# Weighing the values of four query tiles together instead of two, with narrowing matmuls

## Chip, cores and metric

The kernel runs on one core of a Trainium2 chip. The metric is the device time of one execution in microseconds (us), the median of several runs. Engines are named as in the profile: PE (TensorE, matmuls), PEld (its weight loads), DVE (VectorE), ACT (ScalarE), POOL (GpSimd) and SP (SyncE, which issues most DMA transfers).

## What is computed

One layer of a decoder trunk over 1024 tokens of width 1024: a combined input projection, differential attention with 8 heads, a convolution branch, a gated merge and a feed-forward part. The change lies in the attention, whose core is this:

```python
def block(i):                       # 128 queries
    bias = transpose(bias_tab[t5_bucket(rel)], (2, 0, 1))
    causal = rel >= 0
    def probs(qb, kf):
        s = einsum('bhqd,bhkd->bhqk', qb, kf) * scale + bias
        s = where(causal, s, -inf)
        return softmax(s, axis=-1)
    p = probs(qb1, k1f) - lam * probs(qb2, k2f)
    return einsum('bhqk,bhkd->bhqd', p, vf)
...
a = rms_norm(a, subln_w) * (1.0 - lam_init)
y_a = a.reshape(B, S, ATTN_WIDTH) @ w_proj_attn
```

Query tile i (128 queries) sees the key tiles 0 to i only; what lies behind them is masked.

## The kernel before

**Precision.** A product of two fp32 numbers is made in three matmuls: each operand is split into a rounded part ("hi", fp32r) and the rest ("lo"), and `mm3` (lines 168 to 170) adds hi x hi, hi x lo and lo x hi in PSUM. `split_hi` is a copy on ACT (line 120), `split_lo` a subtraction on DVE (line 125).

**The attention stage.** A step is one head h and one query tile i. The 64 steps run head by head, in each of the first seven heads over the tiles 4, 5, 6, 7, 0, 1, 2, 3, and in the last over 6, 7, 4, 5, 2, 3, 0, 1 (`ORDER`). A step n does this:

- `scores` (lines 1289 to 1306): scores of the tile against its keys, bias, exponentials, and the difference of the two softmaxes in the tile E.
- `turn` of the step before: PE transposes E in blocks of 128 x 128 (tile pT), ACT and DVE split the result into ph and pl. ph and pl have one buffer each. A pair of query tiles (b = i // 2) shares them; the block of the pair's last key tile that is masked for the first query tile is set to zero by POOL.
- `weigh`, after the second tile of a pair: V (stationary, 128 x 128, tiles vh and vl) times ph and pl (moving, 256 queries), over 2b + 2 key tiles, into PSUM (pW), and a copy to SBUF by ACT (tile ar).
- `back`, two steps later: PE transposes ar back to queries in rows (pB), and ACT scales it and sums its squares. With the pair that is last in a head, `subln` and, one step on, `subln_T` follow; the result goes to DRAM through the tile "at" (two buffers).
- between them, `more` and `group` issue pieces of the large projections (tile pg; names whi, wlo, hT_hi, hT_lo), which keep PE busy while DVE and ACT work; `turn_qk` turns Q and K of later heads (pQ), whose halves are moved between partitions by DMAs on SP (qs, ks, klo); and one or more convolution taps run on DVE (line 594).

**What sets the order.** The functions are recorded in this order; a scheduler then lists the instructions of each engine, following what depends on what and the explicit `tc.issue_after`. Each engine issues in its listed order. PSUM tiles of the kinds pT, pW, pB, pS and pQ take turns in two pools, `pm` (two buffers) and `pm2` (one buffer).

Of the kernel before, what the change touches and what calls it, by code (L numbers as in the profile page):

```python
# [10 lines left out]
F32 = mybir.dt.float32  # L11
# [5 lines left out]
P = 128  # L17
S = 1024
D = 1024
H = 8  # L20
# [37 lines left out]
def kernel(  # L58
# [28 lines left out]
    dve, act, pool, pe = nc.vector, nc.scalar, nc.gpsimd, nc.tensor  # L87
# [24 lines left out]
    def nm(s):  # L112
        uid[0] += 1
        return f"{s}_{uid[0]}"

    def f32(ap):
        return ap.bitcast(F32)

    def split_hi(dst, src):
        act.copy(dst, src)  # L120
# [3 lines left out]
    def split_lo(dst, src, hi):  # L124
        last_lo[0] = dve.tensor_tensor(dst, src, f32(hi), op=ALU.subtract).ins  # L125
# [9 lines left out]
    def after(ins):  # L135

        return nullcontext() if ins is None else tc.issue_after(ins)

    def last_of(engine):
        for ins in reversed(nc.cur_bb.bb.instructions):  # L140
            if ins.engine == engine:
                return ins
# [19 lines left out]
    def pm(z="pm"):  # L162
        npm[0] += 1
        p_, tag = pms[npm[0] % len(pms)]
        return p_.tile([P, 512], F32, tag=tag, name=nm(z))

    def mm3(o, lh, ll, rh, rl, start, stop):
        pe.matmul(o, lh, rh, start=start, stop=False)  # L168
        pe.matmul(o, lh, rl, start=False, stop=False)  # L169
        last_mm[0] = pe.matmul(o, ll, rh, start=False, stop=stop).ins  # L170
# [47 lines left out]
    at = [0]  # L218
# [556 lines left out]
    def bias_skew(h):  # L775
        pool.dma_start(t_d[h][:], b_d[h : h + 1, :].to_broadcast([P, TL]))
# [89 lines left out]
    def load_bias(h):  # L866
        tb = apl[0].tile([P, S], F32, tag="tb", name=f"tb{h}", bufs=1)
        skew = t_d[h][:].rearrange("p l -> (p l)")[P - 1 : P - 1 + P * (TL - 1)]
        nc.sync.dma_start(tb[:], skew.rearrange("(p l) -> p l", l=TL - 1)[:, :S])
        TB[h] = tb  # L870
# [361 lines left out]
    n = 0  # L1232
# [21 lines left out]
    aps = apl[0]  # L1254
# [4 lines left out]
    V, AN, SSA, PT, ES, RL = {}, {}, {}, {}, {}, {}  # L1259

    def load_v(h):
        vh = aps.tile([P, NT, VD], F32R, tag="vh", name=f"vh{h}", bufs=1)
        vl = aps.tile([P, NT, VD], F32R, tag="vl", name=f"vl{h}", bufs=1)
        for dst, src in ((vh, v_hi[h // 2]), (vl, v_lo[h // 2])):
            nc.sync.dma_start(
                f32(dst[:]),
                src[:, (h % 2) * VD : (h % 2 + 1) * VD].rearrange("(k p) d -> p k d", p=P),
            )
        V[h] = vh, vl
# [39 lines left out]

    ORDER = [(4, 5, 6, 7, 0, 1, 2, 3)] * (H - 1) + [(6, 7, 4, 5, 2, 3, 0, 1)]  # L1310

    def turn(h, i):

        b = i // 2
        if (h, b) not in PT:
            ph = aps.tile([P, NT, 256], F32R, tag="ph", name=nm("ph"), bufs=1)
            pl = aps.tile([P, NT, 256], F32R, tag="pl", name=nm("pl"), bufs=1)
            pool.memset(f32(ph[:, 2 * b + 1, 0:P]), 0.0)
            pool.memset(f32(pl[:, 2 * b + 1, 0:P]), 0.0)
            PT[h, b] = ph, pl  # L1320
        ph, pl = PT[h, b]
        e = ES.pop((h, i))
        qs = slice((i % 2) * P, (i % 2 + 1) * P)
        for k0 in range(0, i + 1, 4):
            n = min(4, i + 1 - k0)
            pt = pm("pT")
            for k in range(n):
                pe.transpose(pt[:, k * P : (k + 1) * P], e[:, (k0 + k) * P : (k0 + k + 1) * P], ident[:])  # L1328
            src = pt[:, : n * P].rearrange("p (k q) -> p k q", q=P)
            split_hi(ph[:, k0 : k0 + n, qs], src)  # L1330
            split_lo(pl[:, k0 : k0 + n, qs], src, ph[:, k0 : k0 + n, qs])

    def weigh(h, b):

        ph, pl = PT.pop((h, b))
        vh, vl = V[h]
        o = pm("pW")
        nkt = 2 * b + 2
        for k in range(nkt):
            mm3(o[:, :256], vh[:, k, :], vl[:, k, :], ph[:, k, :], pl[:, k, :], k == 0, k == nkt - 1)  # L1340
        ar = aps.tile([P, 256], F32, tag="ar", name=nm("ar"), bufs=1)
        act.copy(ar[:], o[:, :256])
        return ar

    def back(h, b, ar):
        pt = pm("pB")
        for e in range(2):
            pe.transpose(pt[:, e * P : (e + 1) * P], ar[:, e * P : (e + 1) * P], ident[:])
        if h not in AN:
            AN[h] = aps.tile([P, NT, VD], F32, tag="an", name=f"an{h}", bufs=1)  # L1350
            SSA[h] = sm.tile([P, NT], F32, tag="ssa", name=nm("ssa"))
        jk = sm.tile([P, VD], F32, tag="jk", name=nm("jk"), bufs=1)
        for e in range(2):
            i = 2 * b + e
            src, r = pt[:, e * P : (e + 1) * P], RL[h][:, i, 0:1]
            act.activation(AN[h][:, i, :], src, AF.Identity, scale=r)
            act.activation(jk[:], src, AF.Square, scale=r, accum_out=SSA[h][:, i : i + 1])

    def subln(h):
        an = AN[h]  # L1360
        r = rstd_of(SSA[h][:], NT, 1.0 / VD, fast=True)
        dve.tensor_tensor(an[:], an[:], r.unsqueeze(2).to_broadcast([P, NT, VD]), op=ALU.mult)

    def subln_T(h):
        an = AN[h]
        for sb in range(2):
            pt = pm("pS")
            for i in range(4):
                pe.transpose(pt[:, i * P : (i + 1) * P], an[:, 4 * sb + i, :], ident[:])
            if h == H - 1:  # L1370

                hi, lo = [a_[-1][:, sb * 512 : (sb + 1) * 512] for a_ in (aT_hi, aT_lo)]
                act.activation(hi, pt[:], AF.Identity, scale=pcol("subln"))
                dve.scalar_tensor_tensor(lo, pt[:], pcol("subln"), f32(hi), op0=ALU.mult, op1=ALU.subtract)
                continue
            at = aps.tile([P, 512], F32, tag="at", name=nm("at"), bufs=2)
            act.activation(at[:], pt[:], AF.Identity, scale=pcol("subln"))
            nc.sync.dma_start(a_d[h][:, sb * 512 : (sb + 1) * 512], at[:])
# [9 lines left out]
    scm, weighs, backs, sublns = [], [], [], []  # L1388
# [3 lines left out]
    def more(k):  # L1392

        with after(scm[-4] if len(scm) >= 4 else None):
            for _ in range(k):
                next(fill, None)
        last_fill[0] = last_mm[0]
# [8 lines left out]
    def ready(queue, n):  # L1406
        now = [e for e in queue if e[0] <= n]
        queue[:] = [e for e in queue if e[0] > n]
        return [e[1] for e in now]

    def slot(n, nq):

        with after(last_fill[0]):
            for h, b, ar in ready(backs, n):
                back(h, b, ar)
                if b == ORDER[h][-1] // 2:
                    subln(h)
                    sublns.append((n + 1, h))
            for _ in range(min(nq, 2)):
                if late[0][0] <= n:  # L1420
                    late.pop(0)[1]()
            for h in ready(sublns, n):
                subln_T(h)
            for h, b in ready(weighs, n):
                backs.append((n + 2, (h, b, weigh(h, b))))
                if b == ORDER[h][-1] // 2 and h + 1 < H:
                    load_v(h + 1)

    def groups(n):

        return 0 if plan[n // NT] == 6 and n % NT in (4, 6) or n == len(steps) - 1 else 1
# [14 lines left out]
    for n, (h, i) in enumerate(steps):  # L1446
        if n % NT == 0 and h:
            load_bias(h)
        if n % NT == 2 and h + 2 < H:
            with after(last_of(mybir.EngineType.Pool)):  # L1450
                bias_skew(h + 2)
        p = groups(n)
        nq = len(late)
        scores(h, i)
        scm.append(last_mm[0])
        more((p + 1) // 2)
        if n:
            hp, ip = steps[n - 1]
            turn(hp, ip)
            if ip % 2:  # L1460
                weighs.append((n, (hp, ip // 2)))
        more(p // 2)
        slot(n, nq)
        due += share * slack[n]
        with after(last_of(mybir.EngineType.DVE)):
            bg.step(int(due + 1e-6))
        due -= int(due + 1e-6)
    n = len(steps)
# [63 lines left out]
    for h in (5, 6):  # L1532
        for sb in range(2):
            cs = slice(sb * 512, (sb + 1) * 512)
            at = bp.tile([P, 512], F32, tag="ya", name=f"at{h}_{sb}", bufs=4)[:]
# [145 lines left out]
    for cl in ((0, 1, 2), (3, 4), (5, 6), (7,)):  # L1681
        pair = [(c, ws.next()) for c in cl]
        for sb in range(2):
            cs = slice(sb * 512, (sb + 1) * 512)
            for c, w in pair:
# [3 lines left out]
                o = gemm_T(w, cT_hi, cT_lo, sb)  # L1689
# [63 lines left out]
    for z, tag in enumerate(("xhi", "xlo")):  # L1753
        t_ = f32(big.tile([P, NKT, S], F32R, tag=tag, name=f"room{z}")[:])
# [37 lines left out]
    o = {}  # L1792
    for z, (z_, b_, s_, (l, c), full) in enumerate(WSEVEN):
# [21 lines left out]
        for j in range(4):  # L1815
# [24 lines left out]
            for i in range(4):  # L1840
                t_ = slice(i * P, (i + 1) * P)
# [17 lines left out]
        for i in range(4):  # L1859
            t_ = 4 * l + i  # L1860
            h = xa[t_][:, TOK[c]]
# [273 lines left out]
```

## Time and profile before

| | us |
|---|---|
| median of 3 runs | 1727.08 |
| lowest and highest run | 1726.94 and 1728.37 |
| span of the profiled execution, first to last instruction | 1725.7 |
| attention stage, about 306 to 822 in the span | 516 |
| PE busy over the span | 1714.6 |
| DVE busy over the span | 1275.4 |
| ACT busy over the span | 862.5 |

The profiled execution has no time of its own beside its span. A row of the groups reads: line, engine, operation, output <- inputs by tile name, shape, count, then total busy us, mean ns of one, and idle time before it with what ended it. A row of the timeline reads: start in us, duration in us, engine, line, operation, names, shape. PE's durations overlap, so that the distance between starts tells what a matmul costs in a stream.

### The profile page before, as it was taken

How to read it: one execution, taken by the hardware profiler on the slowest of the kernel's cores; microseconds unless marked ns; L12 is line 12 of the kernel's file. 1: busy time of each engine (PE TensorE's matmuls, PEld its weight loads, DVE VectorE, ACT ScalarE, POOL GpSimd, SP SyncE). 2: the span in 40 equal slices, each digit the busy share in tenths (PEclk: the TensorE clock that was granted, in tenths of full speed). 3: DMA queues.
4: the chain of work that ended last, by engine and by line, in shares of the span. 5: the costliest groups of instructions: out<-in, count | busy, mean ns of one | idle time of the engine just before them, and what ended most of it. 6: DMA issues, size and time to landing. Idle time of an engine off the chain costs nothing.

```text
span 1725.7 us, 25863 instructions
## 1 busy us (share of the span) xinstructions
PE 1714.6 (99%) x9243; PEld 1477.9 (86%) x9243; DVE 1275.4 (74%) x2128; ACT 862.5 (50%) x1958; POOL 219.1 (13%) x207
## 2 busy tenths in 40 slices
PE   9999999999999999999999999999999999999999
PEld 7997889998998998988788888888888888888887
DVE  7675889898988888878687769966676666575544
ACT  5333335767777776756556325633333333333332
POOL 3997851000000000000000000000000000000000
PEclk9999999999999999999999999999999999999999
DMA  6344445336345344343973683245455445598663
GB/s 208 116 126 132 131 151 154 104 109 171 104 127 147 115 125 138 101 136 130 333 238 118 200 296 119 74 135 164 147 170 170 154 141 164 175 355 285 217 215 130
DMA packets 261604, 281.64 MB, mean 163 GB/s; under 512 B 16546, under 2 KB 181986, under 8 KB 261475
## 3 DMA queue, kind: packets, MB, share of 16 engines
q1 hardware_dynamic: 254160, 267.71, 48.3%
q0 software_dynamic: 5680, 9.39, 2.6%
q10 hardware_dynamic: 1634, 2.89, 0.5%
q8 instruction: 73, 1.20, 0.3%
q14 instruction: 57, 0.46, 0.1%
HBM read 181.84 MB, written 85.50 MB: 155 GB/s over the span
## 4 chain that ended last, share of the span: by engine, by line
PE 92%; DMA 3%; DVE 2%; ACT 1%; issue 1%; POOL 0%; SPq 0%; DVEq 0%; POOLq 0%; ACTq 0%
PE acc L980 29%; PE acc L488 12%; PE pg L168 12%; PE pg L169 12%; PE pg L170 12%; PE wo L1850 3%; PE sc L1290 2%; PE sc L1289 2%; PE pT L1328 2%; PE pg L1106 1%; DVE acc L594 1%; PE pW L168 1%; PE pW L169 1%; PE pW L170 1%; PE pQ L815 1%
## 5 line engine op out<-in xcount | busy, mean ns | idle before, releaser
L594 DVE SCALAR_TENSOR_TENSOR acc<-u,cw,acc 128x1023 f32<-128x1023 f32 (+14 forms) x240 | 303.4, 1264 | 23.2 <-ACT acc L588 20.7
L170 PE MATMUL pg<-whi,hT_lo 128*128 128x256 f32 x704 | 200.2, 285 | 0.0
L168 PE MATMUL pg<-whi,hT_hi 128*128 128x256 f32 x704 | 199.7, 285 | 0.4 <-DVE v L125 0.4
L169 PE MATMUL pg<-wlo,hT_hi 128*128 128x256 f32 x704 | 199.5, 284 | 0.0
L125 DVE TENSOR_TENSOR wlo<-draw,whi 128x1024 fp32r<-128x1024 f32 x75 | 91.7, 1223 | 83.4 <-ACT whi L120 78.9
L120 ACT CAST whi<-draw 128x1024 fp32r<-128x1024 f32 x75 | 79.1, 1055 | 129.5 <-PE acc L488 114.3
L169 PEld LDWEIGHTS pg<-wlo,hT_hi 128*128 128x128 f32 x704 | 134.4, 191 | 1.8
L170 PEld LDWEIGHTS pg<-whi,hT_lo 128*128 128x128 f32 x704 | 134.3, 191 | 1.8
L168 PEld LDWEIGHTS pg<-whi,hT_hi 128*128 128x128 f32 x704 | 134.0, 191 | 2.1 <-DVE v L125 0.6
L120 ACT CAST whi<-wraw 128x1024 fp32r<-128x1024 f32 x90 | 94.7, 1052 | 70.6 <-PE pg L169 32.6
L488 PE MATMUL acc<-wlo,whi 128*128 128x512 f32 x308 | 119.8, 389 | 0.0
L488 PE MATMUL acc<-whi,wlo 128*128 128x512 f32 x308 | 119.8, 389 | 0.0
L1296 ACT ACTIVATE E<-E,mn 128x640 f32<-128x640 f32 (+7 forms) x128 | 99.8, 781 | 30.8 <-DVE mn L1291 29.2
L168 PE MATMUL pg<-hT_hi,whi 128*128 128x512 f32 x288 | 114.4, 397 | 0.1
L169 PE MATMUL pg<-hT_lo,whi 128*128 128x512 f32 x288 | 113.7, 395 | 0.0
L170 PE MATMUL pg<-hT_hi,wlo 128*128 128x512 f32 x288 | 113.7, 395 | 0.0
L120 ACT CAST whi<-s 128x1024 fp32r<-128x1024 f32 x54 | 56.9, 1053 | 104.9 <-PE acc L980 101.8
L125 DVE TENSOR_TENSOR wlo<-wraw,whi 128x1024 fp32r<-128x1024 f32 x75 | 93.3, 1246 | 12.6 <-ACT whi L120 12.3
L1291 DVE CUSTOM_DVE_ANT_0 E<-sc,tb 128x512 f32<-128x512 f32 (+3 forms) x128 | 74.2, 585 | 33.2 <-PE pT L1328 16.1
L980 PE MATMUL acc<-h_hi,whi 128*128 128x512 f32 x240 | 93.4, 389 | 0.0
L980 PE MATMUL acc<-h_lo,whi 128*128 128x512 f32 x240 | 93.4, 389 | 0.0
L980 PE MATMUL acc<-h_hi,wlo 128*128 128x512 f32 x240 | 90.1, 389 | 0.0
(370 smaller groups left out, 4589.7 us busy)
## 6 DMA issues: line engine op xcount, KB each, us to landing
wraw<-in_w_gate_up_dram SPq DMA_DIRECT2D x44, 512.0 KB, 4.7
wraw<-in_w_in_dram SPq DMA_DIRECT2D x38, 512.0 KB, 4.0
qs<-qs SPq DMA_DIRECT2D x96, 128.0 KB, 2.3
wd<-in_w_down_dram SPq DMA_DIRECT2D x44, 256.0 KB, 3.1
tdT<-wd SPq DMA_DIRECT2D x88, 128.0 KB, 4.8
draw<-sdS SPq DMA_DIRECT2D x44, 256.0 KB, 3.7
draw<-tdT SPq DMA_DIRECT2D x44, 256.0 KB, 3.7
wraw<-in_w_in_dram SPq DMA_DIRECT2D x32, 256.0 KB, 3.3
```

The costliest lines, as they stand in the source:

```text
L120: act.copy(dst, src)
L125: last_lo[0] = dve.tensor_tensor(dst, src, f32(hi), op=ALU.subtract).ins
L168: pe.matmul(o, lh, rh, start=start, stop=False)
L169: pe.matmul(o, lh, rl, start=False, stop=False)
L170: last_mm[0] = pe.matmul(o, ll, rh, start=False, stop=stop).ins
L488: m = pe.matmul(o[s_][i][:], l_[:, ts], r_[:, 512:], start=start and j + y_ == 0, stop=j == n - 1 and y_ == 2, skip_group_check=not start,)
L594: dve.scalar_tensor_tensor(a_, us[c][:, : S - n], cw[:, c, t : t + 1], a_, op0=ALU.mult, op1=ALU.add)
L980: last_mm[0] = pe.matmul(o[:], a_[x_][:, k, :], b_[y_][:, k, :], start=start and k + x_ + y_ == 0, stop=k == 3 and x_ == 1, skip_group_che ...
L1289: pe.matmul(o[:, :w], qh[:, qs], k, start=True, stop=False)
L1291: dve.tensor_tensor_reduce(e[:, ks], o[:, :w], tb[:, S - nk + c0 : S - nk + c0 + w], 1.0, mn[:, j : j + 1] if c0 else 3.0e38, ALU.add, ALU ...
L1296: act.activation(e[:, :nk], e[:, :nk], AF.Exp, bias=mn[:, j : j + 1], scale=-1.0, accum_out=l[:, j : j + 1])
L1850: last_mm[0] = pe.matmul(o[s_][i][:], A[u_], B[v_], start=start and j + y_ == 0, stop=j == 3 and y_ == 2, skip_group_check=not start,).ins
```

## The change

For the first seven heads the query tiles 0 to 3 share one ph and one pl, read as 4 key tiles x 512 queries. They are weighed once, after tile 3. Key tile k is seen only by the queries from tile k on, so its matmuls run over 512, 384, 256 and 128 columns and no zeros are needed. The way back is made in two halves, tiles 0 and 1 one step later, 2 and 3 two steps later. The copy of pW goes to a buffer of the tile "at". Tiles 4 to 7, and the last head, stay as they were.

```diff
+    def four(h, i):
+        return i < 4 and h < H - 1
+
     def turn(h, i):
 
-        b = i // 2
+        b = 0 if four(h, i) else i // 2
         if (h, b) not in PT:
             ph = aps.tile([P, NT, 256], F32R, tag="ph", name=nm("ph"), bufs=1)
             pl = aps.tile([P, NT, 256], F32R, tag="pl", name=nm("pl"), bufs=1)
-            pool.memset(f32(ph[:, 2 * b + 1, 0:P]), 0.0)
-            pool.memset(f32(pl[:, 2 * b + 1, 0:P]), 0.0)
+            if four(h, i):
+                ph, pl = [t_[:].rearrange("p k q -> p (k q)").rearrange("p (k q) -> p k q", q=512) for t_ in (ph, pl)]
+            else:
+                pool.memset(f32(ph[:, 2 * b + 1, 0:P]), 0.0)
+                pool.memset(f32(pl[:, 2 * b + 1, 0:P]), 0.0)
             PT[h, b] = ph, pl
         ph, pl = PT[h, b]
         e = ES.pop((h, i))
-        qs = slice((i % 2) * P, (i % 2 + 1) * P)
+        q0 = i if four(h, i) else i % 2
+        qs = slice(q0 * P, (q0 + 1) * P)
...
     def weigh(h, b):
 
-        ph, pl = PT.pop((h, b))
         vh, vl = V[h]
         o = pm("pW")
+        if four(h, 2 * b):
+            ph, pl = PT.pop((h, 0))
+            for k in range(4):
+                qs = slice(k * P, 512)
+                mm3(o[:, qs], vh[:, k, :], vl[:, k, :], ph[:, k, qs], pl[:, k, qs], k == 0, k == 3)
+            ar = aps.tile([P, 512], F32, tag="at", name=nm("ar"), bufs=2)
+            act.copy(ar[:], o[:])
+            return ar
+        ph, pl = PT.pop((h, b))
...
             for h, b in ready(weighs, n):
-                backs.append((n + 2, (h, b, weigh(h, b))))
+                ar = weigh(h, b)
+                if four(h, 2 * b):
+                    backs.append((n + 1, (h, 0, ar[:, 0:256])))
+                    backs.append((n + 2, (h, 1, ar[:, 256:512])))
+                else:
+                    backs.append((n + 2, (h, b, ar)))
...
-            if ip % 2:
+            if ip == 3 or ip % 2 and not four(hp, ip):
                 weighs.append((n, (hp, ip // 2)))
```

What this makes of the order, at two places of the first head. PE before, where the tiles 0 and 1 are weighed (pW_3885), among the scores (sc) of tile 3:

```order
L1289 MATMUL sc_3959<-ks_1_0_3725,qs_1_1_3708 128x512
L168 MATMUL pW_3885<-ph_3808,vh_3156 128x256
L1290 MATMUL sc_3959<-ks_1_0_3725,qs_1_1_3711 128x512
L1289 MATMUL sc_3963<-ks_1_1_3479,qs_1_1_3708 128x128
L1290 MATMUL sc_3963<-ks_1_1_3479,qs_1_1_3711 128x128
L1289 MATMUL sc_3969<-ks_1_0_3726,qs_1_1_3709 128x512
L169 MATMUL pW_3885<-pl_3809,vh_3156 128x256
L170 MATMUL pW_3885<-ph_3808,vl_3157 128x256
L168 MATMUL pW_3885<-ph_3808,vh_3156 128x256
L169 MATMUL pW_3885<-pl_3809,vh_3156 128x256
L170 MATMUL pW_3885<-ph_3808,vl_3157 128x256
L1328 MATMUL pT_3945<-ident,E_3821 128x128 x3
```

PE in the change, where the four tiles are weighed (pW_4065); its first matmul, over ph and 512 columns, stands 18 rows ahead of these:

```order
L169 MATMUL pW_4065<-pl_3809,vh_3156 128x512
L170 MATMUL pW_4065<-ph_3808,vl_3157 128x512
L168 MATMUL pW_4065<-ph_3808,vh_3156 128x384
L169 MATMUL pW_4065<-pl_3809,vh_3156 128x384
L170 MATMUL pW_4065<-ph_3808,vl_3157 128x384
L168 MATMUL pW_4065<-ph_3808,vh_3156 128x256
L169 MATMUL pW_4065<-pl_3809,vh_3156 128x256
L170 MATMUL pW_4065<-ph_3808,vl_3157 128x256
L168 MATMUL pW_4065<-ph_3808,vh_3156 128x128
L169 MATMUL pW_4065<-pl_3809,vh_3156 128x128
L170 MATMUL pW_4065<-ph_3808,vl_3157 128x128
L1289 MATMUL sc_4098<-ks_1_0_3726,qs_1_1_3709 128x512
```

Six matmuls of 256 columns went from the first place, and at the second, where 12 of 256 columns stood before, 12 of four widths stand now. Between the first matmul and these, 17 of a projection (pg) are listed. In all, PE has 42 matmuls fewer: 126 of 256 columns are replaced by 21 each of 512, 384, 256 and 128.

ACT before, from the copy of tiles 0 and 1 (ar_3892) over their way back (pB_4063) to the copy of tiles 2 and 3 (ar_4101):

```order
L1342 COPY ar_3892<-pW_3885 128x256
L120 CAST ph_3941<-pT_3945 128x3x128
L797 COPY qkraw_3995<-pg_4134 128x512
L1296 ACTIVATE E_3958,l_3957<-E_3958,mn_3956 128x640
L120 CAST ph_3941<-pT_4056 128x4x128
L1356 ACTIVATE an_3696<-pB_4063,rl_0_3182 128x128
L1357 ACTIVATE jk_4066,ssa_3697<-pB_4063,rl_0_3182 128x128
```

ACT in the change, from the joint copy to the first half of the way back (pB_4196):

```order
L1350 COPY ar_4078<-pW_4065 128x512
L1296 ACTIVATE E_4087,l_4086<-E_4087,mn_4085 128x768
L120 CAST whi_3976<-wraw_3974 128x1024
L1296 ACTIVATE E_4097,l_4086<-E_4097,mn_4085 128x768
L120 CAST ph_4181<-pT_4185 128x4x128
L120 CAST ph_4181<-pT_4192 128x128
L1371 ACTIVATE an_3696<-pB_4196,rl_0_3182 128x128
L1372 ACTIVATE jk_4199,ssa_3697<-pB_4196,rl_0_3182 128x128
```

One copy of 512 columns stands for two of 256, and the way back of tiles 0 and 1 comes behind the turn of the next head's first tile (pT_4185) instead of behind that of tile 3.

## The prediction

> **What bounds the kernel now.** I read the page first, then the waits of TensorE (PE), then the stage in which the change lies.
>
> ```profile
> span 1725.7 us, 25863 instructions
> PE 1714.6 (99%) x9243; PEld 1477.9 (86%) x9243; DVE 1275.4 (74%) x2128; ACT 862.5 (50%) x1958; POOL 219.1 (13%) x207
> PE   9999999999999999999999999999999999999999
> PEclk9999999999999999999999999999999999999999
> PE 92%; DMA 3%; DVE 2%; ACT 1%; issue 1%; POOL 0%; SPq 0%; DVEq 0%; POOLq 0%; ACTq 0%
> ```
>
> PE is busy in every slice at full clock, and 92% of the chain that ended last is PE. A matmul's busy time includes a modelled end that overlaps the next matmul, so "99%" alone doesn't prove it; the list of what PE waited for does:
>
> ```profile
> PE pm L208 <- DVE busy L195: 1.5, 1, 1.5
> PE sc L1289 <- DMA ks<-klo: 1.1, 1, 1.1
> PE sc L1290 <- DMA qs<-qs: 0.8, 1, 0.8
> PE px L724 <- DVE xt L714: 0.6, 1, 0.6
> ```
>
> The columns are the total wait in us, how often, and the longest. These are the largest; everything else is 0.5 us or less. Only two of them, together 1.9 us, lie in the attention stage:
>
> ```profile
> core 0: us, PE busy (x) PEld busy (x) DVE busy (x) ACT busy (x) POOL busy (x), PEclk, DMA share, GB/s
> 306.00:822.00 516.00, 513.49 (x3417) 468.86 (x3417) 441.57 (x977) 365.38 (x1202) 19.49 (x73) 1.00 0.44 126
> ```
>
> In these 516 us VectorE (DVE) works 441.6 and ScalarE (ACT) 365.4, so both have slack, and PE has next to none. So the time follows the PE work that is issued, counted from one matmul's start to the next one's start, plus any new wait.
>
> **The change, part by part.** First the weighing. Before, each head weighs tiles 0 and 1 with 2 key tiles x 3 = 6 matmuls of 256 columns, and tiles 2 and 3 with 4 x 3 = 12. What one costs:
>
> ```profile
> L168 PE MATMUL pW<-ph,vh 128*128 128x256 f32 x160 | 45.7, 286 | 0.1
> 340.70 0.28 PE L168 MATMUL pW<-ph,vh 128*128 128x256 f32 x1
> 340.82 0.28 PE L169 MATMUL pW<-pl,vh 128*128 128x256 f32 x1
> ...
> 342.74 0.28 PE L170 MATMUL pW<-ph,vl 128*128 128x256 f32 x1
> 342.86 0.60 PE L1328 MATMUL pT<-ident,E 128*128 128x128 f32 x4
> ```
>
> The mean of 286 ns is the time until a result is out, not the price. The 18 matmuls of one weighing start between 340.70 and 342.86: 2.16 us / 18 = 0.120 us each. Removed per head: 18 x 0.120 = **2.16 us**.
>
> The new form has three matmuls each of 512, 384, 256 and 128 columns. pW has none of the other widths, but other matmuls of the same type do:
>
> ```profile
> 929.88 0.39 PE L168 MATMUL pg<-cT_hi,whi 128*128 128x512 f32 x1
> ...
> 932.82 0.39 PE L169 MATMUL pg<-cT_lo,whi 128*128 128x512 f32 x1
> 319.79 0.34 PE L1289 MATMUL sc<-ks,qs 128*128 128x384 f32 x1
> 319.97 0.34 PE L1290 MATMUL sc<-ks,qs 128*128 128x384 f32 x1
> 320.14 0.28 PE L168 MATMUL pg<-whi,hT_hi 128*128 128x256 f32 x1
> 340.02 0.22 PE L1289 MATMUL sc<-ks,qs 128*128 128x128 f32 x1
> 340.08 0.28 PE L1290 MATMUL sc<-ks,qs 128*128 128x128 f32 x1
> 340.19 0.45 PE L168 MATMUL pg<-hT_hi,whi 128*128 128x512 f32 x1
> 340.47 0.39 PE L169 MATMUL pg<-hT_lo,whi 128*128 128x512 f32 x1
> ```
>
> 512 columns: the two rows are the first and the last of 14 in a row, so 2.94 us / 13 = 0.226 us. 384 columns: two take from 319.79 to 320.14, 0.175 us each. 128 columns: the start after the first comes 0.06 us later, but the time is paid afterwards: from the first narrow matmul to the start of the second wide one are 0.45 us; less 0.226 for the wide one between, the two narrow ones take 0.224, **0.112 us each**, nearly what 256 columns cost. The reason is in the weight loads (PEld) of the same place, whose starts stand 0.11 us apart:
>
> ```profile
> 340.02 0.19 PEld L1290 LDWEIGHTS sc<-ks,qs 128*128 128x128 f32 x1
> 340.13 0.19 PEld L168 LDWEIGHTS pg<-hT_hi,whi 128*128 128x128 f32 x1
> 340.24 0.19 PEld L169 LDWEIGHTS pg<-hT_lo,whi 128*128 128x128 f32 x1
> ```
>
> Each matmul here has weights of its own, and a run of narrow ones goes at the pace of the loads. In the changed program the three 128-column matmuls stand one behind the other. So the new weighing costs 3 x (0.226 + 0.175 + 0.120 + 0.112) = **1.90 us** a head. The gain is 2.16 - 1.90 = 0.26 us a head, and 7 heads x 0.26 = **1.8 us**. Bounds for the one disputed price: at 0.06 us a narrow matmul (the first start-to-start above) the gain would be 0.42 a head, 2.9 in all; at 0.120 (no cheaper than 256 columns) 0.24 a head, 1.7 in all. I take 0.112, which the rows give for matmuls in a run.
>
> The Trainium skill ("TensorE: Matmul & The Clock Gate", Back-to-back issue gap) speaks of a sustained roofline of about 81 ns for a matmul of 128 columns and 131 ns for one of 512, weight loads included; with 81 ns the gain would be an estimated 2.4 us in place of 1.8. The trace here disagrees for 512 columns, 226 ns, and shows 112 for the narrow ones in a run. The same page (LDWEIGHTS) puts a load of 128 columns at 128 / 1.2 = 107 ns, which the 0.11 us between the loads above bears out, and which speaks against narrow matmuls as a way to save time.
>
> Next what lies beside PE:
>
> ```profile
> L1342 ACT COPY ar<-pW 128x256 f32<-128x256 f32 x32 | 11.9, 372 | 19.4 <-PE pW L170 19.3
> L797 ACT COPY qkraw<-pg 128x512 f32<-128x512 f32 x27 | 15.9, 588 | 7.8 <-PE pg L170 7.7
> L1318 POOL MEMSET ph<- 128x128 f32 x31 | 6.5, 210 | 0.0
> ```
>
> Two ACT copies of 256 columns (0.74 us) become one of 512 (about 0.59, by the second row): 0.15 us less a head on an engine with 150 us of slack; nothing on the path, as long as PE has its own matmuls between the weighing and the way back. GpSimd loses four 0.2 us memsets a head; it waits nearly all the time. Transposes, their splits on ACT and DVE, and scores are as many as before. Both zero at the sum; if the cover goes, ACT's copy costs at most its 0.59 us a head, 4 in all.
>
> The split of PE work between places: the weighing of 0.72 us behind tile 1 goes, and that behind tile 3 grows from 1.44 to 1.90 us. The first needed the split of tile 1, which is a wait that may vanish, but the list above has no wait of pW over 0.5 us, so it is worth nothing. The second has, in the first head of the new order, 17 other matmuls between its first and its second one, some 2 us (17 x 0.120) in which DVE can finish the low part of tile 3.
>
> The way back of tiles 0 and 1 moves behind the joint weighing, one step later, and that of tiles 2 and 3 stays two steps behind. Its cover in the old order was this:
>
> ```profile
> 555.02 0.37 ACT L1342 COPY ar<-pW 128x256 f32<-128x256 f32 x1 [0.19 <-PE pW L170]
> 557.66 0.38 PE L1348 MATMUL pB<-ident,ar 128*128 128x128 f32 x2
> ```
>
> The copy ends at 555.39, 2.3 us before PE wants it. In the new order some 40 rows, mostly of 256 columns, stand between the last pW and the first pB, about 40 x 0.12 = 4.8 us, and the wider copy takes 0.22 us more. So no wait there, unless ACT is 3 us behind. SSA and the norm come at the same step as before, since the second half of the way back is what closes a head. The "at" ring, now shared, has two buffers for three tiles a head; the new one is free again a step before the third tile asks for it, so I take nothing for it, at most one transfer's delay on ACT.
>
> Against the execution's own 1725.7 us span this gives 1723.9; the span lies 1.4 us under the median of the runs, 1727.08, which I take as what lies around it. 1727.08 - 1.83 = **1725.2 us**.
>
> **Rivals.** (1) *The K and Q of the next head arrive late.* This ends on the slower side. The two waits in the stage are of this kind:
>
> ```profile
> 551.93 0.59 SPq L831 DMA_DIRECT2D qs<-qs  x1
> 555.09 0.46 SPq L832 DMA_DIRECT2D qs<-qs  x1
> 556.92 0.55 SPq L837 DMA_DIRECT2D ks<-klo  x1
> 558.12 0.28 PE L170 MATMUL pg<-whi,hT_lo 128*128 128x256 f32 x1
> 559.47 0.47 PE L1289 MATMUL sc<-ks,qs 128*128 128x512 f32 x1 [1.08 <-DMA ks<-klo]
> ```
>
> PE stands at 558.12 with nothing to issue until the last K transfer has landed; SP issues in order and sat from 551.93 to 555.09 on an earlier one. The change thins the cover: between the last turn of head 4's K and Q and its first score stood 51 matmuls of 256, 9 of 512 and 5 of 128 columns; now 39, 11 and 8, by the prices above 0.65 us less. For head 3 it is 0.6 less, for head 2 0.7 less; for heads 5 and 6 0.2 and 0.5 more. If each of the seven changes of head came to wait 1.1 us as this one does, the stage would lose up to 7 x 1.1 - 1.9 = 5.8 us against now and end at 1725.2 + 5.8 = 1731. It decides from 0.26 us of extra wait a head, which eats the gain. Against it: heads 1, 3, 4, 5 and 6 had 8.0 to 8.8 us of cover by the same count and only two of them waited; the cover stays in that band.
>
> (2) *The same waits vanish.* Heads 4 and 6 keep 8.1 and 8.6 us of cover, and the turn of K no longer queues behind a weighing of tiles 0 and 1. Then 1725.2 - 1.9 = 1723.3.
>
> (3) *Narrow matmuls at the lower bound*, 0.06 us: 1727.1 - 2.9 = 1724.2. The rows speak against it unless other matmuls slip between the three.
>
> (4) *No gain at all*: PE work that isn't the limit. The waits rule out most of it; it would give 1727.1. That the change doesn't do what it says is excluded by the instructions shown above: 42 matmuls fewer, in the widths named.
>
> **How the numbers follow.** A measurement of this kernel can tell about 0.2%, 3.5 us, from no change: faster means under 1723.6, slower over 1730.5. Forecast (1725.2, within 1.2 us of it as waits shift): 0.61. Rival 1: 0.14, of which 0.06 ends over 1730.5. Rival 2: 0.12. Rival 3: 0.05, rival 4: 0.08. Faster 0.13 (rival 2 and a little of 3), slower 0.06, same 0.81. The range takes in rivals 2 to 4 and the nearer half of rival 1, two to three late heads at 1.1 us: 1723.0 to 1728.3.
>
> **What would show it.** Right: 21 pW matmuls of each new width; starts 0.226, 0.175, 0.120 and 0.112 us apart, so one weighing of 1.9 us; the stage about 1.8 us shorter; no PE wait with pW or pB in the list; waits of the first scores of a head around 2 us in total. Wrong: narrow matmuls 0.06 apart to the end of the run (rival 3); waits on K or Q at most heads (rival 1), none (rival 2); a DVE or ACT wait at pW's second matmul or at pB.

## The result and the profile after

The changed kernel is **slower**: 1736.42 us median of 5 runs (1735.33 to 1738.19) against 1726.94 us (1726.01 to 1728.37), ratio 1.0056 with a 95% interval of 1.0044 to 1.0068. The forecast was 1725.2 us with a range of 1723.0 to 1728.3. Medians are over all runs of a kernel; one execution of e2, below, took 9817 us and is left out of its ratio.

The page of the profiled execution after, which is the fastest of the five:

```profile
span 1733.6 us, 25690 instructions
PE 1714.8 (99%) x9201; PEld 1475.6 (85%) x9201; DVE 1278.8 (74%) x2128; ACT 863.5 (50%) x1951; POOL 214.2 (12%) x179
PE 93%; DVE 3%; DMA 2%; ACT 2%; issue 1%; SPq 0%; DVEq 0%
```

PE has 42 matmuls fewer and yet is "busy" for the same time, one more sign that this number is no measure of its work. The span is 7.9 us longer. What PE waited for (total us, times, longest):

```profile
PE pg L168 <- ACT jk L800: 3.3, 2, 2.7
PE sc L1289 <- DVE mn L1291: 2.4, 3, 1.7
PE sc L1289 <- DMA ks<-klo: 1.9, 1, 1.9
PE pm L208 <- DVE busy L195: 1.5, 1, 1.5
PE pg L169 <- DVE aTl L125: 1.3, 2, 0.8
PE pg L168 <- DVE aTl L1389: 1.1, 1, 1.1
```

The two rows at the head are new. The first says that a projection (pg) could not start because ACT had not finished line 800: the squares of the Q and K projection, whose results go to a throwaway tile jk. The largest waits of both rows lie in one place of head 1, in the timeline of PE:

```profile
391.74 0.39 PE L1289 MATMUL sc<-ks,qs 128*128 128x512 f32 x1
391.97 0.40 PE L1290 MATMUL sc<-ks,qs 128*128 128x512 f32 x1
394.10 0.50 PE L1289 MATMUL sc<-ks,qs 128*128 128x512 f32 x1 [1.74 <-DVE mn L1291]
394.44 0.40 PE L1290 MATMUL sc<-ks,qs 128*128 128x512 f32 x1
397.55 0.60 PE L168 MATMUL pg<-hT_hi,whi 128*128 128x512 f32 x1 [2.71 <-ACT jk L800]
397.95 0.63 PE L169 MATMUL pg<-hT_lo,whi 128*128 128x512 f32 x1
398.38 0.63 PE L170 MATMUL pg<-hT_hi,wlo 128*128 128x512 f32 x1
```

Between 391.97 and 397.55 PE starts two matmuls. Then a third loss follows: the 512-column matmuls start 0.42 us apart instead of 0.226. The busy time by stretch shows why; the clock granted to PE is the number behind the POOL entry:

```profile
core 0: us, PE busy (x) PEld busy (x) DVE busy (x) ACT busy (x) POOL busy (x), PEclk, DMA share, GB/s
391.00:394.00 3.00, 1.36 (x7) 0.84 (x5) 3.00 (x9) 3.00 (x11) 0.00 (x0) 1.00 0.58 171
394.00:397.50 3.50, 0.73 (x2) 0.30 (x2) 3.50 (x8) 3.28 (x19) 0.00 (x0) 1.00 0.26 64
397.50:401.00 3.50, 3.45 (x9) 2.67 (x10) 3.25 (x8) 1.19 (x3) 0.00 (x0) 0.54 1.04 348
```

After the pause the clock is at half. Cut finer, it falls at 397.8 and is back at 401.2, 3.4 us later. Eight matmuls at 0.2 us too much are another 1.6 us. From the starts above, less 0.226 us for each matmul, this one place costs 1.9 + 2.9 + 1.6 = 6.4 us.

Why ACT was late is read on ACT. Its timeline, from the copy of that projection to the first and last of its eight squares, and of the next projection the copy (391.93) and the first square (407.67):

```profile
381.43 0.59 ACT L797 COPY qkraw<-pg 128x512 f32<-128x512 f32 x1 [1.31 <-PE pg L170]
383.66 0.59 ACT L1350 COPY ar<-pW 128x512 f32<-128x512 f32 x1 [1.64 <-PE pW L170]
...
388.57 1.05 ACT L120 CAST whi<-wraw 128x1024 fp32r<-128x1024 f32 x1 [3.40 <-PE pg L170]
...
391.34 0.37 ACT L1372 ACTIVATE jk<-pB,rl 128x128 f32<-128x128 f32 x1
...
391.93 0.60 ACT L797 COPY qkraw<-pg 128x512 f32<-128x512 f32 x1
...
393.35 0.41 ACT L1372 ACTIVATE jk<-pB,rl 128x128 f32<-128x128 f32 x1
...
394.73 0.25 ACT L800 ACTIVATE jk<-pg 128x64 f32<-128x64 f32 x1
...
397.18 0.22 ACT L800 ACTIVATE jk<-pg 128x64 f32<-128x64 f32 x1
...
407.67 0.26 ACT L800 ACTIVATE jk<-pg 128x64 f32<-128x64 f32 x1
```

The copy is done at 382.02, and the squares of the same PSUM tile start at 394.73, 12.7 us later, although ACT idles for 3.4 us in between (the row at 388.57). The names tell why: the way back (line 1372) and the squares (line 800) write the same tile **jk**, which has one buffer. The way back was recorded first (jk_4199, the squares jk_4288), so the scheduler, which moved the projection and its copy ahead, could not move the squares. In the listed order of ACT in the changed kernel:

```
L797 COPY qkraw_4236<-pg_4238 128x512
L1350 COPY ar_4078<-pW_4065 128x512
...
L1372 ACTIVATE jk_4199,ssa_3697<-pB_4196,rl_0_3182 128x128
...
L800 ACTIVATE jk_4288,ss_487_4237<-pg_4238 128x64 x8
```

Until the squares are done, pg_4238 holds one of pg's two PSUM buffers. The other holds the next projection, pg_4390, which PE has finished and whose squares come 15.1 us behind their copy. So PE has no projection to fill with. A shorter lag, from the end of the copy to the first square, does not stop PE: the kernel before has lags of up to 8.2 us and no wait of PE on these squares.

### The profile page after: what moved, and what is told of

It reads as the page before. It is cut to its first block, busy times and chain, and to the rows that moved or that the text cites. A ratio compares the mean times of both kernels' runs of the same rounds, so it can differ in the third digit from the quotient of the medians.

```text
span 1733.6 us, 25690 instructions
## 1 busy us (share of the span) xinstructions
PE 1714.8 (99%) x9201; PEld 1475.6 (85%) x9201; DVE 1278.8 (74%) x2128; ACT 863.5 (50%) x1951; POOL 214.2 (12%) x179
## 4 chain that ended last, share of the span: by engine, by line
PE 93%; DVE 3%; DMA 2%; ACT 2%; issue 1%; SPq 0%; DVEq 0%
PE acc L980 30%; PE acc L488 12%; PE pg L168 12%; PE pg L169 12%; PE pg L170 12%; PE wo L1870 3%; PE sc L1289 2%; PE sc L1290 2%; PE pT L1335 2%; DVE acc L594 1%; PE pg L1106 1%; PE pW L169 1%; PE pW L170 1%; PE pW L168 1%; PE pQ L815 1%
## 5 line engine op out<-in xcount | busy, mean ns | idle before, releaser
L125 DVE TENSOR_TENSOR wlo<-wraw,whi 128x1024 fp32r<-128x1024 f32 x75 | 93.6, 1250 | 12.7 <-ACT whi L120 12.1
```

## Experiments

**Theory J:** the joint way back, which comes a step later, holds up the squares through the shared one-buffer tile; the squares hold a buffer of pg; PE runs dry; its clock drops. **Rivals:** the moved way back is bad in itself, the shifted turn of the PSUM pools (25 tiles a head instead of 26, so that the tiles fall into other pools than before), or the narrow matmuls. All times are medians in us beside a kernel before on the same chip, ratios with 95% intervals.

**e1, a throwaway tile of its own for the squares of the projection**, in the changed kernel:

```diff
-jk = sm.tile([P, VD], F32, tag="jk", name=nm("jk"), bufs=1)[:, :HD]
+jk = sm.tile([P, HD], F32, tag="jq", name=nm("jq"), bufs=1)[:]
```

> The change, with a throwaway tile of its own (128x64) for the squares of the Q and K projection, so that they no longer share the one-buffer tile jk with the squares of the way back. Theory J (the shared tile makes the squares of a projection wait for a way back recorded ahead of them; they hold PSUM buffers of pg, PE runs out of work, and the clock drops): the squares follow their copy at once (first square under 3 us behind the copy, where the changed kernel has 12.7 and 15.1 us), PE's waits near 392 to 398 us go, the clock stays at 1.00 there, and 5 to 7 us come back: 1729.5 to 1731.5. Rival S (the order at that place is bad for another reason, the moved way back or the ring of PSUM tiles): the wait stays within 1 us of what it was, 1735 to 1738.

Measured 1725.52 (1724.07 to 1726.70) against 1727.26, ratio 0.9990 (0.9981 to 0.9999); once more, 1725.14 against 1727.08, 0.9988 (0.9978 to 0.9998). All of the loss is gone and more than was expected. ACT's timeline of e1 at the same place, copy and squares:

```profile
381.88 0.59 ACT L797 COPY qkraw<-pg 128x512 f32<-128x512 f32 x1 [1.47 <-PE pg L170]
382.36 0.23 ACT L800 ACTIVATE jq<-pg 128x64 f32<-128x64 f32 x1
...
385.57 0.21 ACT L800 ACTIVATE jq<-pg 128x64 f32<-128x64 f32 x1
...
385.77 0.58 ACT L1350 COPY ar<-pW 128x512 f32<-128x512 f32 x1
```

The squares follow at once, ahead of the copy of pW, and PE's list has no row for these squares any more. In the profiled executions PE's listed waits between 300 and 930 us add up to 10.2 us in the changed kernel and 3.4 in e1; with the 1.6 us at half clock that is 8.4 of the 9.7 us between the two spans. The repeat:

> e1 once more, on the same chip as e10 and e2, so that the three can be set side by side: 1724.5 to 1726.5.

**e2, the same line in the kernel before.**

> The kernel before with the same throwaway tile of its own for the projection's squares. Theory J: the kernel before had lags of 5 to 8 us in its squares but no PE wait from them, so 1725.5 to 1728 (within 1.5 us of before). If the shared tile costs in the kernel before as well, 1722 to 1725.

Measured 1725.10 against 1727.26, ratio 0.9987 (0.9978 to 0.9996); again, beside e1, 1725.41 against 1727.08, 0.9993 (0.9984 to 1.0001).

> e2 once more for its profile (the first profile was of a disturbed execution): 1724 to 1726.5, squares behind their copy at once, PE's waits in the attention stage under 3 us.

So the shared tile probably cost the kernel before some 2 us too (the second interval just reaches 1). The trace of the repeat agrees: the squares follow their copy at once, and PE's waits on transfers of K and Q, 1.9 us in the kernel before, are no longer in its list. With the tile apart the kernel with and the one without the joint weighing differ by 0.4 us one time and by 0.3 the other way the second time: not told apart.

**e3, both halves of the way back two steps behind**, tile shared:

```diff
-backs.append((n + 1, (h, 0, ar[:, 0:256])))
+backs.append((n + 2, (h, 0, ar[:, 0:256])))
```

> The change, with both halves of the way back two steps behind the joint weighing. Theory J: the way back of tiles 0 and 1 no longer stands ahead of the projection pieces of the next step, so the early lags (12.7 us) go but some behind the doubled way back grow; most of the loss goes if the step matters: 1727 to 1733. Rival (the joint weighing itself or its ring of PSUM tiles): 1735 to 1738.

Measured 1739.07 against 1727.26, ratio 1.0071 (1.0055 to 1.0086): no better than the change, where it was expected to be. In head 1 PE no longer waits, although the second projection there lags 19.5 us: the first one's squares follow at once, so only one buffer is held. Other places take over. PE's largest wait, and the stretches around it and around a second place:

```profile
PE sc L1289 <- DMA ks<-klo: 3.1, 1, 3.1
...
559.00:562.40 3.40, 0.77 (x7) 0.56 (x5) 3.17 (x6) 0.62 (x3) 0.00 (x0) 1.00 0.96 279
562.40:569.30 6.90, 6.42 (x26) 6.06 (x27) 3.18 (x8) 2.22 (x10) 0.00 (x0) 0.51 0.08 33
634.10:637.50 3.40, 3.40 (x17) 3.40 (x17) 3.40 (x7) 3.37 (x14) 0.00 (x0) 0.50 0.04 11
```

At 562 K of the next head comes late (K goes through the squares, the norm, the turn and a DMA), and 6.8 us at half clock follow. At 634.1, after PE waits of 0.4 and 1.5 us (for DVE), come another 3.4 us at half clock.

**e5, e3 with the line of e1.**

> The changed kernel with both halves of the way back two steps behind (as in e3) and the projection's squares in a throwaway tile of their own (as in e1). Theory J (the shared tile): where e3 lost 12 us, this loses nothing, 1723.5 to 1728, and the squares follow their copy at once. Rival (a place for the way back is bad in itself): over 1732.

Measured 1726.02 against 1726.79, ratio 1.0002 (0.9990 to 1.0015). One of the ten runs took 1736.06 us at a mean granted clock of 0.998; it has no trace, and its cause stays open. The 12 us that e3 lost are gone, so the place of the way back harms only through the shared tile.

**e4, the turn of the PSUM pools as before**, tile shared:

```diff
             act.copy(ar[:], o[:])
+            npm[0] += 1
             return ar
```

> The change, with the turn of the PSUM pools pm and pm2 advanced by one at each joint weighing, so that the tiles fall into the same pools as before. Rival P (the shifted turn of the PSUM pools costs the time): back to 1725 to 1728. Theory J: the shared throwaway tile still binds, 1731 to 1738, with waits of PE on ACT's squares still in the list.

Measured 1730.62 against 1727.26, ratio 1.0023 (1.0014 to 1.0032): about 6 us better than the change, a little below what theory J had allowed. PE's list:

```profile
PE sc L1289 <- DVE mn L1291: 2.0, 2, 1.2
PE pg L168 <- ACT jk L800: 1.6, 1, 1.6
```

The same two waits stand at the same place, shorter, and no stretch at half clock follows in this execution. With the tile shared, the turn of the pools thus decides over more than half of the loss, by way of the order; by itself it costs nothing that can be measured, as e9 shows.

**e9, e1 and e4 together.**

> The changed kernel with the own throwaway tile and the turn of the PSUM pools as before (e1 and e4 together). Theory J: with the lag gone the pools matter little, within 2 us of e1, 1723.5 to 1727.5. If the pools cost by themselves: 1719 to 1723.

Measured 1724.49 against 1726.79, ratio 0.9989 (0.9979 to 0.9999), within 2 us of e1 as expected. It is the fastest of all by its median, but the ratios of e1 and e2 lie in its interval.

**e6, the kernel before with only the way back of tiles 0 and 1 one step later:**

```diff
+        if b < 2 and h < H - 1:
+            ar = aps.tile([P, 512], F32, tag="at", name=nm("ar"), bufs=2)[:, 0:256]
+            act.copy(ar, o[:, :256])
+            return ar
...
-backs.append((n + 2, (h, b, weigh(h, b))))
+backs.append((n + (3 if b == 0 and h < H - 1 else 2), (h, b, weigh(h, b))))
```

> The kernel before, weighed in pairs, with only the way back of tiles 0 and 1 moved one step later, as the change does (its copies lie in the tile at). Theory J in its strong form (the moved way back alone makes the loss): lags of 6 to 12 us in the squares of head 1 and 1729 to 1734. In its weak form (the moved way back and the order that the joint weighing makes are both needed): 1726 to 1729.

Measured 1725.73 against 1726.79, ratio 0.9995 (0.9986 to 1.0005). This is 0.3 us under the range of the weak form. The strong form falls: the moved way back alone costs nothing. The two projections at this place have their first squares 4 us behind their copies. What is left is the weak form: the way back that hangs on the later, joint weighing, and the order that follows from it.

**e7, the changed kernel, tile shared, but the squares read the copy in SBUF instead of PSUM:**

```diff
-jk, o[:, g * HD : (g + 1) * HD], AF.Square
+jk, raw[:, 2 * i2 + g // 4, g % 4 * HD : (g % 4 + 1) * HD], AF.Square
```

> The changed kernel, tile jk still shared, but the projection's squares read the copy in SBUF (qkraw) instead of PSUM, so that a late square no longer holds a buffer of pg. Theory J with its second link (the harm comes through the held PSUM buffer): the squares may lag as before, but PE's waits on ACT's squares go and 1724 to 1729. If the lag harms in another way (Q and K late): 1731 or more.

Measured 1726.37 against 1726.79, ratio 0.9997 (0.9987 to 1.0006). This is the most telling run. ACT's timeline, copy and first squares, then PE's at the same moment:

```profile
381.94 0.59 ACT L797 COPY qkraw<-pg 128x512 f32<-128x512 f32 x1 [1.12 <-PE pg L170]
...
395.13 0.23 ACT L1372 ACTIVATION_READ_ACCUMULATOR jk<-pB,rl 128x1 f32 x1
395.40 0.26 ACT L800 ACTIVATE jk<-qkraw 128x64 f32<-128x64 f32 x1
```

```profile
391.42 0.40 PE L1289 MATMUL sc<-ks,qs 128*128 128x512 f32 x1
391.66 0.40 PE L1290 MATMUL sc<-ks,qs 128*128 128x512 f32 x1
391.89 0.39 PE L168 MATMUL pg<-hT_hi,whi 128*128 128x512 f32 x1
```

The squares are as late as in the changed kernel (copy done at 382.53, first square at 395.40, 12.9 us), and it doesn't matter: the next projection starts at 391.89 right behind the scores, since its PSUM buffer was free after the copy. PE's waits on the squares and on DVE (mn), 3.3 and 2.4 us in the changed kernel, are both gone from its list. So the harm runs through the held buffer.

**e10, e1 with the joint weighing in 18 matmuls of 256 columns** (and the masked blocks set to zero):

```diff
-            for k in range(4):
-                qs = slice(k * P, 512)
-                mm3(o[:, qs], vh[:, k, :], vl[:, k, :], ph[:, k, qs], pl[:, k, qs], k == 0, k == 3)
+            for c in range(2):
+                qs = slice(256 * c, 256 * c + 256)
+                for k in range(2 * c + 2):
+                    mm3(o[:, qs], vh[:, k, :], vl[:, k, :], ph[:, k, qs], pl[:, k, qs], k == 0, k == 2 * c + 1)
```

> As e1 (joint weighing, own throwaway tile), but in 18 matmuls of 256 columns as the kernel before has them, with the masked blocks zeroed. It prices the narrow form by itself: with the lag out of the way the narrow form should be worth the 1.6 to 1.8 us of the sum, so this is 1.6 to 1.8 us over e1, about 1727. If narrow matmuls gain nothing, equal to e1 within 0.5 us.

Measured 1726.38 against 1725.14 of e1, measured beside it: 1.2 us more. The sign is that of the sum, but the intervals of the two ratios (0.9988 to 1.0006 and 0.9978 to 0.9998) overlap, and the profiled spans differ by 0.3 us only (1724.6 and 1724.3): not told apart.

## Why the prediction was wrong

**The price of the matmuls was right.** PE's timeline of the changed kernel, one joint weighing:

```profile
381.83 0.40 PE L169 MATMUL pW<-pl,vh 128*128 128x512 f32 x1
382.06 0.40 PE L170 MATMUL pW<-ph,vl 128*128 128x512 f32 x1
382.30 0.33 PE L168 MATMUL pW<-ph,vh 128*128 128x384 f32 x1
382.47 0.34 PE L169 MATMUL pW<-pl,vh 128*128 128x384 f32 x1
...
383.18 0.22 PE L168 MATMUL pW<-ph,vh 128*128 128x128 f32 x1
383.24 0.28 PE L169 MATMUL pW<-pl,vh 128*128 128x128 f32 x1
383.35 0.27 PE L170 MATMUL pW<-ph,vl 128*128 128x128 f32 x1
383.46 0.45 PE L1289 MATMUL sc<-ks,qs 128*128 128x512 f32 x1
383.74 0.39 PE L1290 MATMUL sc<-ks,qs 128*128 128x512 f32 x1
```

512 columns cost 0.235 us (two from 381.83 to 382.30), 384 columns 0.17 to 0.18, and from 383.18 to 383.74 three narrow ones and a wide one: 0.56 less 0.226 is 0.334, or 0.111 each, where 0.112 was forecast and the lower bound of 0.06 is out. So the sum of 1.8 us is right for PE's work. No run shows it as time: e1 and e2, and e1 and e10, are not told apart. In the traces PE's listed waits between 300 and 930 us add up to 3.4 and 2.7 us in e1 and its repeat, and to 1.1 us in the repeat of e2. The difference, 2.3 and 1.6 us, is about what the matmuls save.

**The step that failed** is the one on the way back: "So no wait there, unless ACT is 3 us behind", and with it "Both zero at the sum". PE indeed never waited for the way back: no row of its list names pB or pW. I asked only who waits for the way back itself, and not what is held behind it. The squares of the projection were held through a throwaway tile that I took for nothing, since nobody reads it: 12.7 and 15.1 us behind their copies, both buffers of pg with them, and 6.4 us of PE's time lost at that place. They were visible in the order of ACT ahead of the run: the copy of a projection far ahead of its squares, with a way back between. The engine with "150 us of slack" idled while its next useful work was held up, so slack in busy time did not help.

**The rivals.** The first, late K and Q, ended on the slower side too, but it was not this: PE's waits on K and Q add up to 1.9 us in the changed kernel (ks alone) and to 1.9 us before (1.1 for ks, 0.8 for qs). In e3 the wait on ks is larger (3.1 us), and e5 shows that this too goes with the shared tile. The second and third did not come, nor the time of the fourth, 1727.1 us, though with the tile apart no gain is shown either. None of the rivals was a buffer held by another engine's reader, and none had the half clock, which makes a pause of PE dearer than its own length.

**What stays open.** The span is 7.9 us longer although the matmuls save 1.8, so 9.7 us are lost; the place in head 1 accounts for 6.4 of them, which leaves 3.3. The two rows of the tail in the list above (aTl, 2.4 us against 0.2 before) are most of it; the 1.1 us of line 1389 is also there in e1, e5 and e7, which are not slow, and no run took it by itself. The median lies 1.1 us above the profiled execution, and the other four runs have a mean granted clock of 0.997 or 0.998 against its 0.999; they have no trace. That the narrow matmuls are not the cause is shown by e1 and e7, which have them and are not slow. That the order of the joint weighing makes the lag is what e6 leaves, but no run has the joint weighing in wide matmuls with the tile shared; why the scheduler listed the way back so late was not tried.

## What to carry to other kernels

Before work is moved to another step, look for one-buffer tiles that it shares with other work, throwaway outputs above all: they order instructions that have nothing to do with each other, and whatever the held instruction reads stays occupied. Read a PSUM tile for the last time as early as can be, here in its copy, so that a late reader of the copy holds nothing that PE needs. And in a kernel whose matmul engine never pauses, ask of a change first whether it can open one pause of several us, since a saving of 1.8 us in matmuls is small beside it.

## What was not expected of the hardware

In the changed kernel, pauses of PE of 1.9 and 2.9 us with two matmuls between them were followed by 3.4 us at a granted clock of one half, with matmuls of 512 columns starting 0.42 us apart in place of 0.226. In e3 a wait of 3.1 us was followed by 6.8 us at half clock, and waits of 0.4 and 1.5 us by 3.4 us. The clock can fall after PE has started again: by 0.2 us in the changed kernel (397.55 and 397.8) and by 1.1 us at e3's second place (632.95 and 634.1). The Trainium skill ("TensorE: Matmul & The Clock Gate", What's actually happening) tells of a clock that falls to half after an idle window of about 3.4 us and comes back after a busy one; the trace agrees with the half and with the length of the slow stretches, once and twice 3.4 us, and shows that pauses far under 3.4 us, close together, can be enough. They need not be: in e4's profiled execution, with waits of 1.2 and 1.6 us at the place of the changed kernel, the clock stayed at 1.000, while two of its ten runs, 1732.25 and 1734.91 us, have a mean clock of 0.998. What decides is not shown here.
